# The output product of a hybrid conv/attention layer as seven block products per pair of token tiles

## The chip, the cores and the metric

One core of one Trainium2 chip. The metric is the device time of the whole program in microseconds, here the median of three runs. The engines are called as in the profile: PE (TensorE, with PEld for its weight loads), DVE (VectorE), ACT (ScalarE), POOL (GpSimd) and SP (SyncE, which issues most DMAs).

## The reference, cut to what matters

A decoder layer for 1024 tokens of width 1024, in float32. Two branches, a causal convolution and a dilated window attention of 24 heads, are gated and merged, and one output product brings them back to the residual stream.

```python
merged = jax.nn.sigmoid(g_conv) * y_conv + jax.nn.sigmoid(g_att) * y_att   # y_att = (att * silu(z_att)) @ w_att_out
x = x + gate * (merged @ w_o[layer])                                      # 1024 x 1024 x 1024
return _rmsnorm(x, final_g)
```

## The kernel before

All products are made on PE in three matmuls with two-part operands: each float32 operand is split into a high part (`hi`, ACT rounds it to the matmul type) and a low part (`lo`, the rest, by a subtraction on DVE or POOL), and hi.hi, hi.lo and lo.hi are summed in PSUM (`mm3`, L72 to L75). A "group" of twelve such matmuls is four 128-row steps of the contraction at 512 columns.

The program runs in stages. A first stage makes modulation and the first projections. A second makes the other projections, the convolution and its output; there many projections are made in pairs by `strassen` (L703 on), a two by two block product with seven block products for eight: four sums of weight blocks are made by POOL, the sums of the other operand (`t_hi`, `t_lo`) stand ready, and each product's result is passed on by ACT copies from bank to bank. This stage follows an order written out by hand: in each step stand PE's group, then ACT's copies (rank COPY), evictions (EVICT) and high pieces (HIGH), then POOL's pieces (POOLED), then DVE's work on results (POST_), then loads (LOAD). `at(step, rank, fn)` puts work into it. Within a step the ranks come in that order, and within a rank what was put in first comes first. Every engine has its own queue and takes its instructions in the order in which they are written there, the stage's loop being within `tc.manual_schedule`.

The attention stage is likewise written out in slots. One slot is twelve matmuls of a projection (queries, keys, then the last gates) with the attention's own scores, transposes and value products between them; slots -11 to -1 hold projections alone. `move_kq` (L1263) copies query and key parts with DMAs issued by SP into one tile per head; the scores of the first heads are in slot 0. Work beside it stands in `beside`, by slot: loading values, combining the three groups of heads (`combine`), splitting the first blocks of `w_o` (`w_out`) and of `w_att_out` (`first_ao`). `oc` tiles (four buffers) hold the attention's results. The last act ahead of attention is to store `gate_c` as a row (`gscr`, 1024 elements of 4 bytes).

The last stage is not written out in steps before the change; its order is the planner's, by the order of the program. For each of eight tiles `d` of the merged features, `project` makes two groups with the attention output (`ah`, `al`) as the right operand and `w_att_out`'s split columns as the left one; DVE multiplies with the gate `sgr` (Sigmoid by ACT), adds `ttr` (the convolution's share), and the sum is split into `hh[:, d]` (ACT) and `hl[:, d]` (DVE). Then each of eight token tiles `t` gets its 1024 output columns in two halves: `out_cols` makes 24 matmuls over eight contraction steps, DVE multiplies with `gate_b` and adds the tokens' `x`, ACT squares and sums. `out_norm` then works out the row's scale (three small DVE operations, a square root on ACT, five small ones on DVE) and scales two halves, which SP stores. The last tile's second half is done in two quarters of 256 columns.

## Time and profile before

| | us |
|---|---|
| median of 3 runs (1207.93 to 1208.35) | 1208.23 |
| the profiled execution | 1208.01 |
| its span, first to last instruction | 1206.2 |
| merge with the attention output, from PE's first matmul to the output's first | 1067.43 to 1110.95 |
| output product, to PE's last matmul | 1110.95 to 1198.18 |
| end of the span | 1206.2 |

Times in the profile count from the first instruction. A row of the order of time is: start, duration, engine, line, operation, what is written from what, sizes, count, and in brackets how long the engine was idle ahead of it and what released it. A "q" behind an engine is its sequencer, which issues DMAs. The rows of stages give the length, then each engine's busy time and instructions, the granted share of PE's clock, the DMA engines' busy share and the GB/s moved. A row of DMA issues gives count, KB each, and the median time from issue to landing.

### The profile page before, as it was taken

What the parts mean: (1) busy time and instruction counts of PE and PEld (TensorE: products, weight loads), DVE (VectorE), ACT (ScalarE), POOL (GpSimd) and SP (SyncE); (2) the same over time, 40 slices, a digit from 0 to 9 for tenths busy, and PEclk for the clock granted to TensorE, in tenths of its full rate; (3) what the DMA queues carried; (4) which work ended last, traced back from release to release, by engine and by line L of the source; (5) the groups of instructions that cost most, each with busy time, mean ns of one, the idle gap of its engine ahead of it and who ended that gap; (6) DMA issues with size and microseconds to landing.
All of it is one profiled execution on the core that took longest, in us unless ns stands there. A gap on an engine that the chain in (4) does not pass through costs nothing.

```text
span 1206.2 us, 17336 instructions
## 1 busy us (share of the span) xinstructions
PE 1189.1 (99%) x6042; PEld 996.1 (83%) x6042; DVE 905.1 (75%) x1488; ACT 586.7 (49%) x1213; POOL 429.2 (36%) x316
## 2 busy tenths in 40 slices
PE   9999999999999999999999999999999999999997
PEld 7787888888888888788888888888888888888886
DVE  7879999999999998796346657867877852649444
ACT  5655244545444443741126656656656664445111
POOL 0005867787787874672321111111111111200000
PEclk9999999999999999999999999999999999999999
DMA  9685333313233147666855455665666563768232
GB/s 358 192 300 175 105 106 122 101 66 105 100 100 131 63 140 274 226 201 235 225 135 149 111 144 130 181 174 141 180 168 146 145 191 124 234 228 281 87 105 70
DMA packets 100141, 194.49 MB, mean 161 GB/s; under 512 B 29587, under 2 KB 43219, under 8 KB 100054
## 3 DMA queue, kind: packets, MB, share of 16 engines
q1 hardware_dynamic: 83376, 186.77, 50.4%
q10 hardware_dynamic: 16678, 6.61, 2.0%
q8 instruction: 48, 0.79, 0.3%
q14 instruction: 39, 0.32, 0.1%
HBM read 122.25 MB, written 39.62 MB: 134 GB/s over the span
## 4 chain that ended last, share of the span: by engine, by line
PE 90%; DVE 3%; ACT 2%; DMA 2%; issue 1%; POOL 1%; SPq 0%; DVEq 0%; ACTq 0%; POOLq 0%
PE d L73 23%; PE d L74 23%; PE d L75 23%; PE o L1370 4%; PE d L603 4%; PE s L1333 3%; PE t L1349 3%; PE d L1661 2%; PE d L1662 2%; PE d L1663 2%; DMA wraw<-in_w_v 1%; PE d L274 1%; ACT hh L238 1%; DVE hl L241 1%; DVE tot L788 1%
## 5 line engine op out<-in xcount | busy, mean ns | idle before, releaser
L545 DVE SCALAR_TENSOR_TENSOR acc<-u,cw,acc 128x1024 f32<-128x1024 f32 x232 | 298.8, 1288 | 6.6
L73 PE MATMUL d<-hh,whi 128*128 128x512 f32 x752 | 295.0, 392 | 2.2 <-ACT gs L1023 2.2
L74 PE MATMUL d<-hl,whi 128*128 128x512 f32 x752 | 293.4, 390 | 0.0
L75 PE MATMUL d<-hh,wlo 128*128 128x512 f32 x752 | 293.3, 390 | 0.0
L456 POOL TENSOR_TENSOR wlo<-wraw,whi 128x512 fp32r<-128x512 f32 x130 | 175.8, 1362 | 216.4 <-ACT whi L453 216.2
L58 POOL TENSOR_TENSOR wlo<-wraw,whi 128x512 fp32r<-128x512 f32 (+1 forms) x56 | 82.9, 1498 | 366.5 <-ACT whi L57 362.5
L75 PEld LDWEIGHTS d<-hh,wlo 128*128 128x128 f32 x752 | 141.2, 188 | 30.2
L73 PEld LDWEIGHTS d<-hh,whi 128*128 128x128 f32 x752 | 141.4, 188 | 29.1 <-ACT gs L1023 2.7
L74 PEld LDWEIGHTS d<-hl,whi 128*128 128x128 f32 x752 | 141.4, 188 | 25.9
L453 ACT ACTIVATE whi<-wraw 128x512 fp32r<-128x512 f32 x130 | 79.1, 624 | 86.9 <-DMA wraw<-in_w_co 26.1
L1342 ACT ACTIVATE sb<-sb,stats 128x128 f32<-128x128 f32 (+1 forms) x192 | 84.8, 443 | 31.2 <-DVE stats L1338 30.9
L1338 DVE CUSTOM_DVE_ANT_0 sb<-s,mask 128x128 f32<-128x128 f32 (+1 forms) x192 | 59.7, 349 | 52.9 <-PE s L1333 51.5
L1349 PE MATMUL t<-ident,sb 128*128 128x128 f32 x280 | 73.7, 276 | 0.0
L1370 PE MATMUL o<-ph,vt 128*64 128x128 f32 (+1 forms) x432 | 65.9, 253 | 0.0
L1164 ACT ACTIVATE ph<-t 128x384 fp32r<-128x384 f32 (+2 forms) x96 | 45.6, 475 | 38.9 <-PE t L1349 25.8
L1167 DVE TENSOR_TENSOR pl<-t,ph 128x384 fp32r<-128x384 f32 (+2 forms) x96 | 52.0, 541 | 10.8 <-ACT ph L1164 10.2
L1333 PE MATMUL s<-k,ql 128*128 128x128 f32 (+1 forms) x192 | 55.0, 292 | 0.0
L1164 ACT ACTIVATE kqp<-rot 128x512 fp32r<-128x512 f32 x24 | 23.1, 964 | 64.4 <-DVE rot L1187 39.0
L1370 PE MATMUL o<-pl,vt 128*64 128x128 f32 (+1 forms) x216 | 52.8, 261 | 0.0
L1661 PE MATMUL d<-oh,hh 128*128 128x512 f32 (+1 forms) x136 | 51.2, 377 | 0.0
L1663 PE MATMUL d<-oh,hl 128*128 128x512 f32 (+1 forms) x136 | 51.2, 377 | 0.0
L73 PE MATMUL d<-uh,whi 128*128 128x512 f32 x128 | 50.0, 390 | 1.2 <-ACT gs L612 1.2
(300 smaller groups left out, 2640.2 us busy)
## 6 DMA issues: line engine op xcount, KB each, us to landing
wraw<-in_w_t SPq DMA_DIRECT2D x67, 512.0 KB, 4.2
k<-kqp SPq DMA_DIRECT2D x96, 128.0 KB, 2.3
q<-kqp SPq DMA_DIRECT2D x96, 128.0 KB, 2.3
wraw<-in_w_v SPq DMA_DIRECT2D x19, 512.0 KB, 4.5
wa<-in_w_ada SPq DMA_DIRECT2D x16, 512.0 KB, 5.8
ql<-kqp SPq DMA_DIRECT2D x48, 128.0 KB, 2.3
wg<-wscr SPq DMA_DIRECT2D x48, 128.0 KB, 3.2
hscr<-x SPq DMA_DIRECT2D x8, 512.0 KB, 3.4
```

Source lines behind the costliest of these rows:

```text
L58: (lo_eng or nc.vector).tensor_sub(lo, raw, hi.bitcast(F32))
L73: nc.tensor.matmul(ps, lh, rh, start=start, stop=False, skip_group_check=again)
L74: nc.tensor.matmul(ps, lh, rl, start=False, stop=False, skip_group_check=again)
L75: nc.tensor.matmul(ps, ll, rh, start=False, stop=stop, skip_group_check=again)
L453: nc.scalar.activation(self.hi, src(), AF.Copy)
L456: nc.gpsimd.tensor_sub(self.lo, src(), self.hi.bitcast(F32))
L545: nc.vector.scalar_tensor_tensor(acc, u[:, k:k + S], cw[:, ct, k:k + 1], acc, op0=mult, op1=add)
L1333: products.append((w, lambda c=c, w=w, l=x[:, ts_], r=k[:, ks], i=i: nc.tensor.matmul(ps[:, c:c + w], l, r, start=i == 0, stop=i == 1)))
L1342: nc.scalar.activation(sb[:, c:c + w], sb[:, c:c + w], AF.Exp, bias=stats[:, t, h, 1:2], scale=-1.0, accum_out=stats[:, t, h, 0:1])
L1349: yield from ((lambda c=c: nc.tensor.transpose(ps[:, c:c + P], sb[:, c:c + P], ident)) for c in range(0, o, P))
L1370: nc.tensor.matmul(out_, l, r, **kw))
L1661: nc.tensor.matmul(ps, hh[:, k, c], rh, start=k == 0, stop=False)
```

## The change

The last stage becomes a second run of the hand-written steps (`serve_steps`, the old loop as a function). Steps 0 to 15 are the merge's groups, as before in count, but the merged features are kept whole in `merged[0]` and `merged[1]` and not split. Steps 16 to 43 are four pairs of token tiles (t, t + 4), each with seven block products of twelve matmuls in place of eight: blocks are two tiles of tokens by two halves of the contraction by two halves of the columns. The sums of merged blocks are made in place, in the first pair by DVE, in the others by POOL, and split piece by piece (`Form2`). The four sums of `w_o` blocks are made early in attention (`out_combos`: loads, one DVE, three POOL operations, one ACT negation, stores to `tscr`, for each of two halves), loaded again in the merge and split by ACT and POOL into `hh` and `hl`. Two blocks of `w_o` are split late, in steps 16 and 17 (`late_b`). In attention the fourth block of `w_o` is now split as well (slot 113), and the first two column blocks of `w_att_out` are loaded.

```diff
+    def out_combos(c):
+        t = b11, b12, b22, b21 = [ap_.tile([P, S], F32, name="oc", tag="oc", bufs=4) for _ in range(4)]
+        for x, n, kp in zip(t, (0, 1, 1, 0), (c, c, 2 + c, 2 + c)):
+            nc.sync.dma_start(x, a["w_o"][n, kp])
+        nc.gpsimd.tensor_sub(b11, b11, b12)
+        yield
+        nc.vector.tensor_sub(b12, b12, b22)
+        nc.gpsimd.tensor_add(b22, b22, b11)
+        nc.gpsimd.tensor_sub(b21, b21, b22)
+        yield
+        for x, i in ((b11, 0), (b12, 2)):
+            nc.sync.dma_start(tscr[i][c], x)
+        yield
+        nc.scalar.activation(b22, b22, AF.Copy, scale=-1.0)
+        for x, i in ((b22, 1), (b21, 3)):
+            nc.sync.dma_start(tscr[i][c], x)
         yield
...
-                  (110, w_out(0, 2)), (111, first_ao())):
+                  (110, w_out(0, 2)), (111, first_ao()), (113, w_out(0, 3))):
         in_steps(it, [x, x + 2])
+    in_steps(out_combos(0), [-11, -8, -4, -2])
+    in_steps(out_combos(1), [-1, 2, 4, 6])
...
+    def merge(d, half):
+        s = cols_of(half)
+        ps = bank()
+        for k in range(4):
+            c = slice(k * P, (k + 1) * P)
+            mm3(ps, ao[d].hi[:, c], ao[d].lo[:, c], ah[k][:, s], al[k][:, s], k == 0, k == 3)
+
+        def post():
+            m = merged[d // 4][:, d % 4, s]
+            nc.vector.tensor_mul(sg[d][:, s], ps, sg[d][:, s])
+            nc.vector.tensor_add(m, m, sg[d][:, s])
+        at(now[0], POST_, post)
...
+        at(max(2 * d - 2, -1), LOAD, lambda d=d: sg_load(d))
+        at(max(2 * d - 4, -1), LOAD, lambda d=d: merged_load(d))
+        at(2 * d, EVICT, lambda d=d: nc.scalar.activation(sg[d], sg[d], AF.Sigmoid))
...
+    for step, i, c, tag in ((0, 1, 0, "wlo"), (1, 1, 1, "wlo"), (3, 2, 0, "wraw"), (5, 2, 1, "wraw"), (7, 3, 0, "wlo"),
+                            (9, 3, 1, "wlo"), (11, 4, 0, "wraw"), (12, 4, 1, "wraw")):
+        combo(step, i, c, tag)
+
+    def late_b(step, c):
...
+        def high():
+            woh[1, 2 + c], wol[1, 2 + c] = (head_tile(x, "oh") for x in (("k0", "k1"), ("k2", "q0"))[c])
+            nc.scalar.activation(woh[1, 2 + c], raw[0], AF.Copy)
+        at(step, LOAD, load)
+        at(OUT + c, HIGH, high)
+        at(OUT + c, POOLED, lambda: nc.gpsimd.tensor_sub(wol[1, 2 + c], raw[0], woh[1, 2 + c].bitcast(F32)))
+
+    for c in range(2):
+        late_b(13 + 2 * c, c)
...
+    def out_pair(p):
+        step = OUT + 7 * p
+        rows = [slice(t * P, t * P + P) for t in (p, p + 4)]
+        a11, a12, a21, a22 = (merged[kh][:, :, r] for r in rows for kh in range(2))
...
+            def __init__(self, n, src, high_at, low_at, eng):
+                def high():
+                    tag = ("wlo", "wlo", "whi", "whi", "wraw", "wraw", "wraw")[n]
+                    Pieces.__init__(self, wpool.tile([P, 1024], F32R, name="wf", tag=tag,
+                                                     bufs=3 if tag == "wraw" else 2))
+                    nc.scalar.activation(v(self.hi), src(), AF.Copy)
+                at(high_at, HIGH, high)
+                at(low_at, POST_ if eng is nc.vector else POOLED,
+                   lambda: eng.tensor_sub(v(self.lo), src(), v(self.hi).bitcast(F32)))
...
+        if first_:
+            f11 = Form2(0, lambda: a11, 12, 12, P_)
+            at(step - 1, POST_, lambda: D_.tensor_add(v(s1), a21, a22))
+            fs1 = Form2(1, lambda: v(s1), step, step, D_)
+            at(step, POST_, lambda: D_.tensor_add(a21, a21, a11))
+            at(step, POST_, lambda: D_.tensor_add(a11, a11, v(s1)))
+            fs2 = Form2(2, lambda: a11, step + 1, step + 1, D_)
+            f12 = Form2(3, lambda: a12, step + 1, step + 1, D_)
+            at(step + 1, POOLED, lambda: P_.tensor_add(v(s4()), a12, a11))
+            fs3 = Form2(4, lambda: a21, step + 2, step + 2, D_)
+            fs4 = Form2(5, lambda: v(s4()), step + 3, step + 3, P_)
+            f22 = Form2(6, lambda: a22, step + 4, step + 4, P_)
+        else:
+            at(step - 3, POOLED, lambda: P_.tensor_add(v(s1), a21, a22))
+            f11 = Form2(0, lambda: a11, step - 3, step - 2, P_)
+            at(step - 2, POOLED, lambda: P_.tensor_add(a21, a21, a11))
+            at(step - 2, POOLED, lambda: P_.tensor_add(a11, a11, v(s1)))
+            fs1 = Form2(1, lambda: v(s1), step - 2, step - 1, P_)
...
+            f22 = Form2(6, lambda: a22, step + 3, step + 4, P_)
...
+        t1, t2 = p, p + 4
+        end = p == 3
+        at(step, COPY, copy("b", "a"))
+        at(step + 1, COPY, copy("x", "g", 1.0, 0))
+        at(step + 2, COPY, copy("d", "b", -1.0))
+        at(step + 3, POST_, lambda: gated(t1, 0, 0, 512, box["a"]))
+        at(step + 4, COPY, copy("y", "d", 1.0, 1))
+        at(step + 5, POST_, lambda: gated(t2, 1, 512, 1024, box["g"], ((box["y"], box["g"]), sub)))
+        at(step + 5 + (not end), POST_, lambda: gated(t1, 1, 512, 1024, box["b"], ((box["b"], box["x"]), add)))
+        at(step + 5 + 2 * (not end), POST_, lambda: out_norm(t1, 2))
...
+        at(step + 6, POST_, whole)
+        at(step + 6 + (not end), POST_, lambda: out_norm(t2, 3 if end else 2))
+        groups.extend([g0, g1, more("b", fs2, combo_block(2)), more("a", f12, b_block(0, 1)),
+                       more("d", fs3, combo_block(3)), more("b", fs4, b_block(1, 1)),
+                       last if end else more("d", f22, combo_block(4))])
```

`gated` is two DVE operations (multiply with `gate_b`, add to `x` in place), three where a result is first the sum or difference of two, and ACT's sum of squares. `last` makes the last block product in two halves of 256 columns, and `whole` for the last pair takes each half by itself.

More of the change, by code (lines that the diff above doesn't have):

```diff
@@ L102, in layer @@
     vcscr = [dram.tile([P, S], F32, name=f"vcscr{j}") for j in range(KT)]
+    tscr = [[dram.tile([P, S], F32, name=f"tscr{i}{c}") for c in range(2)] for i in range(4)]
     szscr = [dram.tile([P, S], F32, name=f"szscr{j}") for j in range(KT)]
@@ new lines, in layer, with ao_load, ao_high @@
+    ao = {0: Pieces(ahead_ao[0])}
+    raw_ao = {d: ahead_ao[1][:, d * 512:d * 512 + 512] for d in range(2)}
+    def ao_load(d, tag):
+        raw = in_half(tag, "raws")
+        for i in range(2):
+            raw_ao[d + i] = raw[:, i * 512:i * 512 + 512]
+            nc.sync.dma_start(raw_ao[d + i], a["w_ao"][d + i])
+    def ao_high(d):
+        late = {2: hh[:, 6], 3: hh[:, 7], 4: hl[:, 6], 5: hl[:, 7]}
+        ao[d] = Pieces(late[d] if d in late else wpool.tile([P, 1024], F32R, name="whi", tag="whi"))
+        ao[d].high(raw_ao[d])
@@ new lines, in layer @@
+    for d in range(KT):
+        for half in (range(2) if d < KT - 1 else (1, 0)):
+            groups.append(lambda d=d, half=half: merge(d, half))
+        at(max(2 * d - 2, -1), LOAD, lambda d=d: sg_load(d))
+        at(max(2 * d - 4, -1), LOAD, lambda d=d: merged_load(d))
+        at(2 * d, EVICT, lambda d=d: nc.scalar.activation(sg[d], sg[d], AF.Sigmoid))
+    at(-1, LOAD, lambda: ao_load(2, "gate_b"))
+    at(-1, LOAD, lambda: ao_load(4, "fg_b"))
+    at(5, LOAD, lambda: ao_load(6, "gate_b"))
@@ L1695 @@
+    for p in range(4):
+        out_pair(p)
+    serve_steps(groups)
 def kernel(**inputs):
```

259 lines of the change are left out of this document (160 added, 99 removed).

## The prediction

> **What bounds the kernel now.** I read the page first: its busy shares and the chain that ended last. Then the busy time by stage, TensorE's order of time at the stage borders, and last the other engines' order of time where the change puts work.
>
> ```profile
> span 1206.2 us, 17336 instructions
> PE 1189.1 (99%) x6042; PEld 996.1 (83%) x6042; DVE 905.1 (75%) x1488; ACT 586.7 (49%) x1213; POOL 429.2 (36%) x316
> PE 90%; DVE 3%; ACT 2%; DMA 2%; issue 1%; POOL 1%; SPq 0%; DVEq 0%; ACTq 0%; POOLq 0%
> L73 PE MATMUL d<-hh,whi 128*128 128x512 f32 x752 | 295.0, 392 | 2.2 <-ACT gs L1023 2.2
> ```
>
> TensorE (PE) is the chain. What it does not have to do comes off the time, and every wait put on it is paid in full.
>
> ```profile
> core 0: us, PE busy (x) PEld busy (x) DVE busy (x) ACT busy (x) POOL busy (x), PEclk, DMA share, GB/s
> 1067.43:1110.95 43.52, 43.52 (x194) 36.04 (x192) 34.16 (x53) 25.57 (x35) 0.00 (x0) 1.00 0.89 304
> 1110.95:1195.42 84.47, 84.47 (x385) 70.44 (x384) 42.85 (x100) 15.28 (x41) 0.00 (x0) 1.00 0.28 93
> ...
> 1110.95 0.39 PE L1661 MATMUL d<-oh,hh 128*128 128x512 f32 x1
> 1195.42 0.28 PE L1661 MATMUL d<-oh,hh 128*128 128x256 f32 x1
> ```
>
> The first row is the merge with the attention output (192 matmuls), the second the output product up to its last 24 pieces. In the new stage groups 0 to 15 are merge and 16 to 43 are the four pairs' seven block products each. Both have no idle PE. 43.52 us / 192 = 0.2267 us from matmul to matmul (a matmul's own 0.39 us overlaps the next), so a group of twelve is 2.72 us.
>
> **The change, part by part.**
>
> *Fewer products.* From 1067.43 to the start of the last 24 half-width pieces at 1195.42 PE now takes 127.99 us. Afterwards there lie 16 merge groups and 27 of 28 block groups before the last, again halved, group: 43 x 2.72 = 116.96 us. **-11.03 us**. I call the start of that last group T.
>
> *Waits in the first token pair.* The steps are written out in order: in each, PE's group, then ACT's COPY, then its HIGH pieces. Rows of two earlier stages price this.
>
> ```profile
> 205.24 0.39 PE L73 MATMUL d<-hh,whi 128*128 128x512 f32 x1
> 205.44 0.60 ACT L736 ACTIVATE sd<-d 128x512 f32<-128x512 f32 x1 [1.60 <-PE d L75]
> 205.93 0.62 ACT L453 ACTIVATE whi<-wraw 128x512 fp32r<-128x512 f32 x1
> ...
> 346.16 1.28 POOL L456 TENSOR_TENSOR wlo<-s,whi 128x512 fp32r<-128x512 f32 x1
> 347.49 0.50 PE L75 MATMUL d<-t1h,wlo 128*128 128x512 f32 x1 [0.20 <-POOL wlo L456]
> 347.83 0.40 PE L73 MATMUL d<-t1h,whi 128*128 128x512 f32 x1
> 348.06 0.39 PE L74 MATMUL d<-t1l,whi 128*128 128x512 f32 x1
> ...
> 1057.75 1.06 ACT L1164 ACTIVATE oh<-wraw 128x1024 fp32r<-128x1024 f32 x1 [0.40 <-ACT gs L1204]
> 1058.71 0.62 ACT L1164 ACTIVATE whi<-wraw 128x512 fp32r<-128x512 f32 x1
> 1067.45 0.63 ACT L57 ACTIVATE whi<-wraw 128x512 fp32r<-128x512 f32 x1 [1.41 <-PE d L74]
> 1068.11 0.69 DVE L58 TENSOR_TENSOR wlo<-wraw,whi 128x512 fp32r<-128x512 f32 x1 [0.81 <-ACT whi L57]
> ```
>
> ACT sat 1.60 us for PE at the copy and only then ran the piece written behind it: it keeps the written order. In step 16 of the new stage that order is: copy of `a` into `b` (waits for group 16), `late_b(0)`'s 1024-wide piece, then `fs1`'s high piece. Group 17, next on PE, needs `fs1`. Counted from the moment G when group 17 could start: copy at G+0.20 (205.44 against 205.24), next instruction +0.49, behind the 1024-wide piece +0.96, DVE's low piece +0.66, its end +0.69 = G+3.00. The group's first two matmuls read the high piece and can go earlier; the third needs the low one. A late low piece costs as in the rows at 347.49: PE goes 0.05 after it (346.16+1.28), and the next matmul is 0.34 behind instead of 0.23. The third would have been at G+0.45, so the group ends 3.05-0.45+0.11 = 2.71 us late. Step 17 repeats it: copy of `g`, `late_b(1)`, `fs2`, then DVE; group 18 needs `fs2`. **+5.42 us** for the two. If matmuls waited for the whole tile it would be 0.9 more; if ACT's order were otherwise, 0. Groups 19 to 22 have their pieces: `f12` is done with `fs2`; `fs3` is ready 2.0 us after group 18, needed after 2.7.
>
> *GpSimd before the second pair.* `f22`'s high piece stands behind the copy of `d` in step 20, and six GpSimd operations follow, the last the low piece of the second pair's `fs1`.
>
> ```profile
> 206.05 1.29 POOL L710 TENSOR_TENSOR s<-wraw 128x512 f32<-128x512 f32 x1
> 211.18 1.30 POOL L456 TENSOR_TENSOR wlo<-s,whi 128x512 fp32r<-128x512 f32 x1
> ```
>
> Four starts apart, (211.18-206.05)/4 = 1.28 us each. From step 20's start: 2.72+0.20+0.49+0.63 = 4.04, six operations to 11.7; group 24's third matmul is due at 4 x 2.72+0.45 = 11.33. **+0.5 us** (0, to 1.9 if each took a fifth longer, an estimate). Later pairs put `f22` four microseconds earlier and do not meet this.
>
> *The clock.* Each of those waits leaves PE idle for 2.1 us (G+0.23 to G+2.3) and thin for 0.7 more.
>
> ```profile
> 493.84:497.25 3.41, 3.05 (x22) 2.84 (x22) 1.01 (x5) 1.50 (x4) 2.67 (x2) 1.00 0.94 314
> 497.25:500.67 3.42, 3.42 (x11) 2.64 (x10) 0.34 (x2) 1.88 (x4) 1.97 (x2) 0.50 0.96 369
> ```
>
> This is the one drop of the granted clock inside the trace: after a stretch of 3.41 us with one gap and a few tiny matmuls (x22 in all) the next 3.42 us ran at 0.50, which costs up to 1.7 us. I take one drop out of two waits: **+1.7 us** (0 to 3.4). The Trainium skill (TensorE: Matmul & The Clock Gate, "Why this matters for your kernels") allows gaps up to about 3 us: only "One MID window of idle" brings half clock. By that rule neither wait would drop it and the sum would be 1.7 lower. The trace's drop came with PE at work for part of the window, so the row speaks against a rule that wants it wholly idle.
>
> *The tail.* In the last pair DVE's order is: the gated block of tile 7, the one of tile 3, tile 3's whole norm, then only the two halves that PE finishes last.
>
> ```profile
> 1187.31 0.69 DVE L1664 TENSOR_TENSOR y<-d,gate_b 128x512 f32<-128x512 f32 x1 [4.02 <-PE d L1663]
> 1188.03 0.69 DVE L1665 TENSOR_TENSOR y<-y,xt 128x512 f32<-128x512 f32 x1
> 1189.51 0.16 DVE L1672 TENSOR_TENSOR r<-ss 128x1 f32<-128x1 f32 x1 [0.79 <-ACT xt L1666]
> 1191.16 1.41 DVE L1679 SCALAR_TENSOR_TENSOR y<-y,r,fg_b 128x512 f32<-128x512 f32 x2
> ...
> 1192.32 0.39 PE L1663 MATMUL d<-oh,hl 128*128 128x512 f32 x1
> 1192.75 0.69 DVE L1664 TENSOR_TENSOR y<-d,gate_b 128x512 f32<-128x512 f32 x1 [0.17 <-PE d L1663]
> ...
> 1198.50 0.42 DVE L1664 TENSOR_TENSOR y<-d,gate_b 128x256 f32<-128x256 f32 x1 [1.26 <-PE d L1663]
> 1198.95 0.42 DVE L1665 TENSOR_TENSOR y<-y,xt 128x256 f32<-128x256 f32 x1
> 1199.95 0.16 DVE L1674 TENSOR_TENSOR r<-r,ss 128x1 f32<-128x1 f32 x1 [0.57 <-ACT xt L1666]
> ```
>
> Tile 3's `b` is done with group 42: DVE follows its last matmul by 0.43 (1192.32 to 1192.75), T+0.20. Three dependent operations 0.72 apart (1187.31 to 1188.03) put the add at T+1.64; the sum of squares is read 1.48 later (T+3.12); the norm takes 3.06 (1189.51 to 1192.57): T+6.18. Then two multiplies and two adds of 256, 0.45 apart, last add at T+7.53; 1.00 to the sum, and 6.25 from there to the end of the span (1199.95 to 1206.2): T+14.78. Now it is 1206.2-1195.42 = 10.78. **+4.00 us**.
>
> *Attention.* Added: eight loads and eight stores of 512 KB, two 1024-wide operations on DVE, six on GpSimd, two on ACT, all early; `w_o`'s fourth block is split inside attention instead of behind it. PE waits for none of it as long as the first heads' moves keep their reserve (rival below). Taken at 0 (0 to 3.4).
>
> *Merge.* DVE loses the splits. The loads grow to 31 of 512 KB, 16.3 MB in about 46 us; the merge row shows 304 GB/s at a DMA share of 0.89, 342 at full share, 47.5 us. So gates come up to 2 us late, but eight banks let PE run eight groups (21.8 us) ahead of DVE, and weights lead by four groups. At the start the second weight tile's piece stands behind the first Sigmoid; 0, at most the 2.2 us that the L73 row lost at its one such place.
>
> **Sum.** -11.03+5.42+0.5+1.7+4.00 = +0.6 on the profiled execution's 1208.01 (span 1206.2 and 1.81 around it), 1208.6; the median of the runs shown is 0.22 above that execution: **1208.8 us**, no change.
>
> **Rivals.**
>
> *Faster, the waits do not come:* ACT takes the pieces before the copies, or the groups find them ready. 1208.8-5.42-1.7 = **1201.7 us**. Against it: the 1.60 us in the row at 205.44, with the piece behind it.
>
> *The clock holds in both waits* (above): 1208.8-1.7 = **1207.1 us**, inside the forecast case, with a quarter of its chance, since the one drop seen does not say how idle a window must be.
>
> *Slower, attention's start:*
>
> ```profile
> cscr<-gs SPq DMA_DIRECT2D x2, 256.0 KB, 9.6
> gscr<-gate_c SPq DMA_DIRECT2D x1, 4.0 KB, 11.8
> ql<-kqp SPq DMA_DIRECT2D x4, 128.0 KB, 2.3
> 613.23 0.69 DVE L1167 TENSOR_TENSOR kqp<-rot,kqp 128x512 fp32r<-128x512 f32 x1 [0.70 <-ACT kqp L1164]
> 615.96 0.69 DVE L1167 TENSOR_TENSOR kqp<-d,kqp 128x512 fp32r<-128x512 f32 x1 [2.04 <-ACT kqp L1164]
> 623.95 0.59 SPq L1263 DMA_DIRECT2D ql<-kqp  x1
> 631.46 0.22 PE L1333 MATMUL s<-k,q 128*128 128x128 f32 x1
> ```
>
> The first four weight loads (2.1 MB, 6.1 us at 342 GB/s) stand behind the stores and the 4-byte scatter of `gate_c`, which lands only after 11.8 us. If they land past 614, DVE's subtraction, written ahead of the low piece at 613.23, holds it to 616. The moves behind it go 2.8 us later, with two stores (about 1 us of SP's queue, as its issues beside them, and 3.1 us of DMA) put before the second ones: 6.9 against a reserve of 631.46-(623.95+2.3) = 5.2. PE waits 1.7 us, and as much again where the second set does it in slot 2: **1212.2 us**. It decides when the subtraction waits over 1 us. For it: the 11.8. Against it: DVE's idle 2.04 behind, and the loads may get past the scatter.
>
> That the products do not get fewer is excluded by the listing: seven groups of twelve matmuls per pair; and the block products of the earlier stage run at the same spacing (347.83 to 348.06).
>
> **How the numbers follow.** Forecast case 0.55, its own range 1206.3 to 1211.8 (clock 0 to 3.4, GpSimd 0 to 1.8, the whole-tile wait); faster rival 0.25; slower rival 0.20. A run tells 0.2% (2.4 us) from nothing. Of the forecast case 0.40 lies within that, 0.13 above, 0.02 below: faster 0.27, same 0.40, slower 0.33. The range 1201.5 to 1213.0 takes in both rivals' values.
>
> **What would show it.** In the changed profile: 16 merge groups without a gap, then two gaps of some 2 to 3 us on PE in the first pair, released by ACT and DVE; a third below 1 us at group 24; the clock at 0.50 once behind them; from PE's last matmul to the end about 4 us more than now, with DVE in tile 3's norm when PE stops; no PE gap in attention. A first pair without gaps makes me wrong by 5 to 7 us; a gap at the first scores by 2 to 4.

## The result, and the profile after

The changed kernel takes 1240.6 us (median of four runs, 1237.3 to 1243.4), the kernel before beside it 1208.1: ratio 1.0268, 95% interval 1.0238 to 1.0297. The prediction was 1208.8. The profiled executions took 1237.34 us (span 1235.5) and 1208.01 (span 1206.2), 29.3 apart in span. Runs disturbed as a whole are left out of all comparisons; the profile of one run below (the sums alone, first time) was such a one, at 3088 us, and is not read.

Three lines of the changed kernel's page: span, busy shares, chain.

```profile
span 1235.5 us, 17394 instructions
PE 1190.4 (96%) x5982; PEld 991.9 (80%) x5982; DVE 943.6 (76%) x1478; ACT 608.0 (49%) x1249; POOL 538.7 (44%) x376
PE 76%; DMA 6%; DVE 5%; POOL 4%; issue 4%; ACT 3%; SPq 1%; DVEq 0%; POOLq 0%; ACTq 0%
```

TensorE has 60 matmuls fewer (5982 for 6042), but of the chain it holds 76% where it held 90%. Busy time by stage of the changed kernel: first scores to merge, merge, output blocks up to the last matmul, tail.

```profile
631.81:1075.00 443.19, 438.00 (x2709) 379.17 (x2708) 294.82 (x781) 263.69 (x705) 78.46 (x51) 1.00 0.62 169
1075.00:1118.52 43.52, 43.52 (x193) 36.06 (x192) 29.76 (x28) 19.83 (x24) 28.85 (x14) 1.00 0.92 338
1118.52:1222.84 104.32, 87.98 (x348) 68.64 (x347) 75.40 (x103) 39.99 (x84) 66.49 (x41) 0.89 0.24 84
1222.84:1235.52 12.68, 0.28 (x3) 0.07 (x1) 6.72 (x23) 1.98 (x8) 0.00 (x0) 0.68 0.22 83
```

The merge is as long as before (43.52). The output stage has 104.32 us in place of 87.23, although 28 groups need only 28 x 2.72 = 76.2: 28.1 us are waits and half clock. Attention is 7.2 us longer (443.19 for 435.97), the tail 4.6 (12.68 for 8.04). With 0.4 at the first scores that is 7.2+17.1+4.6+0.4 = 29.3.

By groups (from first matmul to first matmul, less 2.72) the 28.1 us lie at 16 to 18 (15.2), 24 (4.3 with its neighbour), 33 and 34 (3.7), 38 to 41 (4.8). TensorE's waits by what ended them (total, times, longest), from 600 us on:

```profile
PE d L75 <- DVE wf L1821: 5.5, 2, 4.1
PE t L1351 <- DVE pl L1169: 4.9, 2, 4.1
PE d L73 <- ACT wf L1818: 4.9, 2, 2.7
PE d L75 <- POOL wf L1821: 3.4, 3, 2.1
PE d L73 <- ACT d L1855: 2.5, 3, 1.3
PE d L75 <- POOL wlo L58: 2.3, 1, 2.3
```

`wf` are the pieces of the block products and `d` from ACT the copies: 16.3 us of waits in the output stage. What that stage lost beyond them is mostly the clock, below. `pl` lies in attention, where TensorE was also busy 2.0 us longer at half clock (438.00 for 435.97). `wlo` came near 621, ahead of the first scores. That these are only 0.4 us late is luck: the half clock that the trace of before has at 497.25 did not come in this execution. One hundred matmuls ahead of the first scores it lay 2.2 us in front (606.55 for 608.79), and it lost 2.6 us from there on.

### The profile page after: what moved, and what is told of

It reads as the page before. It is cut to its first block, busy times and chain, and to the rows that moved or that the text cites. A ratio compares the mean times of both kernels' runs of the same rounds, so it can differ in the third digit from the quotient of the medians.

```text
span 1235.5 us, 17394 instructions
## 1 busy us (share of the span) xinstructions
PE 1190.4 (96%) x5982; PEld 991.9 (80%) x5982; DVE 943.6 (76%) x1478; ACT 608.0 (49%) x1249; POOL 538.7 (44%) x376
## 4 chain that ended last, share of the span: by engine, by line
PE 76%; DMA 6%; DVE 5%; POOL 4%; issue 4%; ACT 3%; SPq 1%; DVEq 0%; POOLq 0%; ACTq 0%
PE d L75 20%; PE d L73 20%; PE d L74 20%; PE d L604 6%; PE o L1372 4%; PE s L1335 3%; PE t L1351 2%; POOL wf L1821 2%; DMA sgr<-ascr 1%; DVE merged L1692 1%; DMA oc<-in_w_o 1%; DMA ascr<-gs 1%; DMA wraw<-in_w_t 1%; DMA x<-in_xT 1%; DMA tscr<-oc 1%
## 5 line engine op out<-in xcount | busy, mean ns | idle before, releaser
L73 PE MATMUL d<-hh,whi 128*128 128x512 f32 x752 | 295.7, 393 | 2.5 <-ACT gs L1024 2.2
L73 PEld LDWEIGHTS d<-hh,whi 128*128 128x128 f32 x752 | 141.7, 188 | 29.6 <-ACT gs L1024 2.7
L1335 PE MATMUL s<-k,q 128*128 128x128 f32 (+1 forms) x192 | 51.3, 273 | 0.0
L73 PE MATMUL d<-uh,whi 128*128 128x512 f32 x128 | 50.0, 390 | 1.2 <-ACT gs L613 1.2
L604 PE MATMUL d<-whi,hh 128*128 128x512 f32 x128 | 50.5, 394 | 0.0
```

The costliest lines, as they stand in the source:

```text
L73: nc.tensor.matmul(ps, lh, rh, start=start, stop=False, skip_group_check=again)
L604: nc.tensor.matmul(ps[i], l[:, k, c], r, start=k == 0 and n == 0, stop=k == KT - 1 and n == 2)
L1335: products.append((w, lambda c=c, w=w, l=x[:, ts_], r=k[:, ks], i=i: nc.tensor.matmul(ps[:, c:c + w], l, r, start=i == 0, stop=i == 1)))
```

## The experiments

Five theories: A, ACT's written order in steps 16 and 17 (the prediction's); B, DVE and GpSimd hold each other up; C, the early sums block queues at attention's start; F, the square root of a pair's second norm stands ahead of ACT's copies; G, the same of ACT's squares. The table has the profiled executions: start of the merge; what is lost from there to the last group beyond 2.72 us a group; tail. The merge of kernels with the same attention began at 1075.0 to 1081.6, so that column is good to some 6 us, the other two to about 1. A part of this scatter is a wait for `pl` near 985 that some executions have and others not: e14, whose attention is that of the kernel before, loses 5.2 us there, e13 5.1, the changed kernel 1.0, the kernel before nothing. A profiled execution can lie 4 us off the median of its kernel; e12's is the fastest of twelve (1204.7).

| run | time | ratio (95%) | merge begins | lost in groups | tail |
|---|---|---|---|---|---|
| before | 1208.1 | | 1067.4 | 0 | 8.0 |
| after | 1240.6 | 1.0238-1.0297 | 1075.0 | 28.1 | 12.7 |
| e1, e13 sums alone | 1218.7, 1220.9 | 1.0052-1.0100, 1.0063-1.0125 | 1082.7 (e13) | 1.7 (e13) | 8.0 |
| e2 ACT's order | 1235.4 | 1.0189-1.0237 | 1080.8 | 20.4 | 12.9 |
| e3 GpSimd quiet | 1236.2 | 1.0194-1.0241 | 1077.9 | 24.8 | 12.5 |
| e4 both | 1228.4 | 1.0139-1.0219 | 1077.6 | 15.8 | 13.2 |
| e6 second norm later | 1247.3 | 1.0294-1.0335 | 1081.3 | 32.7 | 13.2 |
| e11 and squares later | 1245.1 | 1.0262-1.0320 | 1081.6 | 30.4 | 12.9 |
| e7 tail | 1241.0 | 1.0227-1.0276 | 1077.8 | 30.9 | 11.6 |
| e5 sums on DVE | 1250.1 | 1.0317-1.0356 | 1088.3 | 25.7 | 13.1 |
| e10 sums at the end | 1243.6 | 1.0260-1.0323 | 1068.8 | 37.9 | 12.8 |
| e8 together | 1236.3 | 1.0204-1.0242 | 1085.7 | 17.2 | 11.8 |
| e9 second version | 1221.4 | 1.0091-1.0130 | 1069.8 | 15.5 | 12.1 |
| e12 third version | 1208.8 | 0.9981-1.0002 | 1069.6 | 1.4 | 12.2 |
| e15 last version | 1206.0 | 0.9949-0.9980 | 1069.0 | 5.3 | 10.5 |
| e14 GpSimd beside | 1234.7 | 1.0189-1.0218 | 1072.6 | (other kernel) | 8.0 |

### The first pair: e2, e3, e4

Order of time on ACT, on DVE and on GpSimd around group 17 of the changed kernel:

```profile
1118.08 1.06 ACT L1700 ACTIVATE sgr<-sgr 128x1024 f32<-128x1024 f32 x1 [3.49 <-DMA sgr<-ascr]
1119.04 1.99 ACT L1715 ACTIVATE hh<-wt 128x1024 fp32r<-128x1024 f32 x2
1121.44 0.58 ACT L1855 ACTIVATE d<-d 128x512 f32<-128x512 f32 x1 [0.40 <-PE d L75]
1121.93 1.05 ACT L1731 ACTIVATE oh<-wt 128x1024 fp32r<-128x1024 f32 x1
1123.45 0.63 ACT L1818 ACTIVATE wf<-s 128x512 fp32r<-128x512 f32 x1 [0.47 <-DVE s L1829]
```

```profile
1120.62 2.74 DVE L1829 TENSOR_TENSOR s<-merged,merged 128x512 f32<-128x512 f32 x1
1123.28 0.68 DVE L1691 TENSOR_TENSOR sgr<-d,sgr 128x512 f32<-128x512 f32 x1
1123.99 2.13 DVE L1692 TENSOR_TENSOR merged<-merged,sgr 128x512 f32<-128x512 f32 x1
1126.04 2.82 DVE L1821 TENSOR_TENSOR wf<-s,wf 128x512 fp32r<-128x512 f32 x1
```

```profile
1120.16 5.41 POOL L1716 TENSOR_TENSOR hl<-wt,hh 128x1024 fp32r<-128x1024 f32 x2 [1.64 <-ACT hh L1715]
1125.53 2.79 POOL L1734 TENSOR_TENSOR oh<-wt,oh 128x1024 fp32r<-128x1024 f32 x1
```

ACT's order is the predicted one: copy, 1024-wide piece, `fs1`. But the piece then waits another 0.47 us for the sum `s`, and DVE, which should need 0.69 for each of its operations, takes 2.74, 2.13 and 2.82 for three of them, all with two inputs in SBUF and all beside GpSimd's large subtractions; the one with an input in PSUM (`d`) takes 0.68. And the last gate came late (ACT's Sigmoid waited 3.49 us for its load), so that DVE began late. The third matmul of group 17 started at 1128.92. With 0.69 for each of the three operations, the low piece of `fs1` would by these rows have ended near 1124.2, late gate or not (an estimate); group 17 could start at 1121.24, so that is the prediction's G+3.00. It ended at 1128.86.

e2, theory A:

```
-            fs1 = Form2(1, lambda: v(s1), step, step, D_)
+            fs1 = Form2(1, lambda: v(s1), step, step, D_, EARLY)     # fs2 in the same way
-        at(OUT + c, HIGH, high)                                     # late_b, and its low piece
+        at(OUT + 2 + c, HIGH, high)
```

> The changed kernel with another written order on ScalarE in steps 16 and 17: the high pieces of fs1 and fs2 stand ahead of the copy that waits for TensorE, and the two 1024-wide pieces (late_b) come two steps later. Theory A, ScalarE's order makes the loss of 15.3 us in groups 17 and 18: 9 to 13 of it go, time 1228 to 1232 against 1240.6. Theory B, VectorE and GpSimd holding each other up makes most of it: 2 to 5 go, 1236 to 1239. Groups 24, 34 and 41 keep their 4 us each under both.

e3, theory B (the same in `late_b`, for steps 18 and 19):

```
-        at(step + 3, POOLED, lambda: nc.gpsimd.tensor_sub(hl[:, n], ...))   # the last sum's two
+            last_in((14, 17)[c], lambda: nc.vector.tensor_sub(hl[:, n], ...))
```

> The changed kernel with the low pieces of the last sum (two) and of late_b (two) made by VectorE, behind its other work of steps 14 and 17 to 19, so that GpSimd has next to nothing in steps 14 to 17; ScalarE's order is as in the changed kernel. Theory B: VectorE's adds and low pieces go from 2.1 to 2.8 us back to 0.69, and 6 to 10 of the 15.3 us in groups 17 and 18 go: 1231 to 1235. Theory A: the waits stay, 0 to 3 go: 1238 to 1241.

e4, both edits:

> Both edits together. If A and B between them are the cause, groups 17 and 18 lose under 3 us in place of 15.3: 1227 to 1229. If the gate that comes late from DRAM sets group 17 (ScalarE's last sigmoid waited 3.49 us for it), some 4 us of it stay: 1230 to 1233.

Groups 16 to 18 lose 15.2 us in the changed kernel, 6.7 in e2, 12.9 in e3, 5.9 in e4; over all groups the losses fall by 7.7, 3.3 and 12.3. e2 stayed below the nine of theory A and e3 below the six of theory B; e3's 2.3 us in groups 16 to 18 are what A had foretold for it. And e2 is not A alone, since GpSimd's low pieces of `late_b` move away from group 17 with ACT's. B's price itself did go in e3, on DVE as foretold; what ate the gain is the last gate, on ACT:

```profile
1128.64 0.69 DVE L1835 TENSOR_TENSOR s<-merged,merged 128x512 f32<-128x512 f32 x1
```

```profile
1123.96 1.06 ACT L1700 ACTIVATE sgr<-sgr 128x1024 f32<-128x1024 f32 x1 [5.07 <-DMA sgr<-ascr]
```

This Sigmoid started 46.0 us after the merge's start, in the changed kernel 43.1. Besides, e3 and e4 gave DVE a low piece in step 14 whose high piece ACT makes only behind that Sigmoid, and the gate's multiplication stands behind it: it starts 2.2 us after the Sigmoid's end (1127.19 in e3, 1124.41 in e4), in the changed kernel at once. So A and B are both at work, but these runs do not divide the 15.2 us between them. In e4 5.9 us stay, as the expectation's second half had it, though the time, 1228.4, lies in the range of its first.

### The price of DVE and GpSimd together: e14

```
+        for _ in range(4):
+            nc.gpsimd.tensor_sub(probe[0], probe[0], probe[0])     # in out_cols of the kernel before
```

> The kernel before with 68 subtractions of a 128x512 tile from itself on GpSimd, which nothing needs, beside merge and output stage: the disputed price by itself. Theory B (GpSimd and VectorE hold each other up where both read two operands from SBUF): VectorE's y<-y,xt goes from 0.69 to between 1.2 and 2.2 us in the mean, its y<-d,gate_b with one operand from PSUM stays at 0.69, GpSimd's own operation goes from 1.28 to 1.5 to 1.8. TensorE has all its data early there, so the time stays within 3 us of 1208. Rival (VectorE is slow through DMA writes or ScalarE): both stay at 0.69.

GpSimd could start on these subtractions as soon as their tile was there, and did at 1058.9. So most of the 68 ran beside the merge, and `y<-y,xt` of the output product, which the expectation names, met few (723 ns in the mean there). The merge has an operation of the same kind, `ttr<-ttr,sgr`. DVE's operations by line (count | busy us, mean ns) in the merge of the kernel before, then of e14, then e14's on GpSimd:

```profile
L1633 DVE TENSOR_TENSOR sgr<-d,sgr 128x512 f32<-128x512 f32 x15 | 9.9, 685 | 3.5 <-ACT sgr L1618 3.5
L1634 DVE TENSOR_TENSOR ttr<-ttr,sgr 128x512 f32<-128x512 f32 x14 | 9.2, 684 | 0.0
```

```profile
L1634 DVE TENSOR_TENSOR ttr<-ttr,sgr 128x512 f32<-128x512 f32 x12 | 17.6, 1487 | 0.0
L1633 DVE TENSOR_TENSOR sgr<-d,sgr 128x512 f32<-128x512 f32 x12 | 7.9, 678 | 3.6 <-ACT sgr L1618 3.6
```

```profile
L1660 POOL TENSOR_TENSOR probe<-probe 128x512 f32<-128x512 f32 x44 | 59.4, 1350 | 3.5
```

The operation with both inputs in SBUF goes from 684 to 1487 ns; the one that reads `d` from PSUM stays (685, 678). GpSimd loses little in the mean (1350 ns, not the 1.5 to 1.8 us expected; 1.28 us was the row in the prediction). So B's price on DVE is shown by itself. What I had expected of the time was wrong: 1208 within 3, and it is 1234.7. The kernel before was not safe from it, since DVE, which makes the merge's weight pieces, was busy for 34.16 of its 43.52 us: slowed down, it became the bound there. TensorE waited 12.3 us for its `wlo`, and 5.6 at the start of the output product for `hh` and `hl`.

The Trainium skill (SBUF — State Buffer, "SBUF: two separate sides") gives the reason: the port pair that the two engines share is "an exclusive lock, not a bandwidth split", held for a whole instruction, and on DVE's side an operation with two SBUF inputs wants it when GpSimd's reads SBUF. The rows agree: two SBUF inputs 684 to 1487 ns, one of two in PSUM 685 to 678.

### Groups 33 to 42: e6 and e11

ACT and DVE ahead of group 34 of the changed kernel:

```profile
1186.41 0.20 ACT L113 ACTIVATE tmp<-r 128x1 f32<-128x1 f32 x1 [4.71 <-DVE r L1780]
1186.52 0.58 ACT L1855 ACTIVATE xy<-d 128x512 f32<-128x512 f32 x1
```

```profile
1181.93 1.05 DVE L115 TENSOR_TENSOR tmp<-tmp 128x1 f32<-128x1 f32 x1
1183.02 1.21 DVE L116 TENSOR_TENSOR tmp<-tmp,r 128x1 f32<-128x1 f32 x1
```

ACT stood 4.71 us at the square root of the second tile's norm; the copy behind it was due long before. DVE had been held up in the first tile's norm, even in operations on one column, 1.05 and 1.21 us for what takes 0.16.

```
-        at(step + 6 + (not end), POST_, lambda: out_norm(t2, 3 if end else 2))
+        at(step + (6 if end else 9), POST_, lambda: out_norm(t2, 3 if end else 2))
```

> The changed kernel with the norm of each pair's second tile two steps later (three pairs), so that ScalarE's square root for it no longer stands ahead of the copies of the next pair. Theory F (that square root, waiting 4.7 us for VectorE, makes the waits at groups 33, 34, 40 and 41): 5 to 7 of their 7.8 us go, 1233 to 1236. Rival (GpSimd's chain of pieces alone makes them late): the waits stay, 1240.

The waits at 33, 34, 40 and 41 went as F says; but new ones came at 28, 31, 35, 36 and 42, 11.6 us from 28 to 42 in place of 8.5, and the time is 1247.3 (in the profile 6.3 us of that lie ahead of the merge, in the scatter above). F names the wait and not the cause: the next thing on ACT that waits for DVE took its place. e11 moves that too, the squares:

```
+        if t % 4 < 3:
+            at(now[0] + 1, POST_, square)      # the sum of squares of gated, one step later
```

> The run with the second norm later, and now the squares of the first three pairs one step later too (and with them the first tile's norm). Theory G: in the run before it ScalarE's squares, which wait for VectorE's adds that GpSimd stretches to 1.66 us, stood ahead of the copies in place of the square root; the waits at groups 28 to 42 (11.3 us there, 8.5 in the changed kernel) fall to 2 to 4, time 1236 to 1240 with that run's other waits. Rival: the copies are late through the pieces (GpSimd): 9 to 12 us stay, 1245 to 1248.

Groups 28 to 36 then lose nothing; 6.1 us stay at 37 to 42, most of them at 42, in the last pair, whose squares were not moved. G holds for the pairs in which it was tried; in all, groups 28 to 42 fall from 11.6 to 6.1 us and not to the 2 to 4 expected. The time (1245.1, interval overlapping e6's) does not show it, since the first pair lost 3 us more and the rest of the runs scatters.

### Attention: e1, e13, e5, e10

SP's queue in the changed kernel, what ACT then waits for, what TensorE waits for, SP's raw weights in the kernel before, and GpSimd and TensorE ahead of the first scores:

```profile
631.30 0.80 SPq L1534 DMA_DIRECT2D tscr<-oc  x2
632.15 5.85 SPq L1522 DMA_DIRECT2D oc<-in_w_o  x4
638.05 0.90 SPq L62 DMA_DIRECT2D wraw<-in_w_t  x2
```

```profile
645.77 0.63 ACT L57 ACTIVATE whi<-wraw 128x512 fp32r<-128x512 f32 x1 [5.21 <-DMA wraw<-in_w_t]
```

```profile
649.76 0.30 PE L1351 MATMUL t<-ident,sb 128*128 128x128 f32 x1 [4.09 <-DVE pl L1169]
```

```profile
629.42 1.23 SPq L62 DMA_DIRECT2D wraw<-in_w_t  x2
```

```profile
617.58 2.37 POOL L1527 TENSOR_TENSOR oc<-oc 128x1024 f32<-128x1024 f32 x1
621.21 0.50 PE L75 MATMUL d<-hh,wlo 128*128 128x512 f32 x1 [2.26 <-POOL wlo L58]
```

SP sends its DMAs in the order written. The second set's loads need buffers that the first set's stores must leave first; SP stood 5.85 us over four of them, and the heads' raw weights went out at 638.05 in place of 629.42. ACT, in order too, stood 5.21 us at their split with the softmax pieces behind it, so TensorE waited 4.09 us at the transposes. Ahead of the first scores it waited another 2.26 us for GpSimd, whose split stood behind its sum `oc<-oc`. This wait came in each of the six other executions with the same attention (2.29 to 3.60 us in e2, e3, e4, e6, e7 and e11), in five of them with half clock behind it, and their first scores came at 634.8 to 638.5 (before 631.46).

e1 is the kernel before with nothing but `out_combos` and its slots; e13 is the same once more.

> The kernel before, with nothing of the change but the early sums of output weights in attention (their loads, their adds on GpSimd, VectorE and ScalarE, their stores); the sums are then not used. Theory C, the sums delay attention (SyncE's queue holds the next raw weights behind the sums' stores and loads, GpSimd's split waits behind the sums): attention is 7.6 us longer, the time is 1215 to 1217. Rival: attention is longer through the other edits there (output weights split earlier, the wider first w_ao tile): 1208.

> The run of the early sums alone once more, for its trace (the first one's profiled execution lay at 3088 us, with every matmul at twice its length). Theory C: PE waits near 618 and 645 as in the changed kernel, the merge begins 7 to 11 us later than in the kernel before (1067.4), merge and output stage are as before: 1215 to 1219. Rival, that the sums' data traffic lengthens the later stages: merge and output stage longer than 43.5 and 87.2.

The sums alone cost 0.5 to 1.3%, about 10 us (1218.7 beside 1209.0, 1220.9 beside 1209.2): C, both a little above their ranges. In e13 the same two waits come (2.3 us at GpSimd's split, 2.1 at `pl`), and merge and output stage stay within 1.8 us. Its merge begins 15.2 us late and not 7 to 11: 5.1 of them are lost near 985, in the wait that e14 has without any sums.

e5 makes all sums on DVE and finishes both sets ahead of the raw weights:

```
-        nc.gpsimd.tensor_add(b22, b22, b11)
+        nc.vector.tensor_add(b22, b22, b11)       # and so for all four, and the sign
-    in_steps(out_combos(1), [-1, 2, 4, 6])
+    in_steps(out_combos(1), [-6, -4, -3, -2, -1])
```

> The changed kernel with the early sums of weights made by VectorE alone (the sign too, which ScalarE changed) and their stores and the second set's loads done before SyncE comes to the raw weights of the heads. Theory C (GpSimd's sums ahead of its split, SyncE's queue ahead of the raw weights): PE's waits of 2.65 us near 618 and 4.31 us near 645 go, from the first scores to the merge it is again 436 us in place of 443, time 1232 to 1234 against 1240.6. Rival: the weight traffic itself delays the heads' weights wherever the sums are made: the waits stay within 2 us, 1238 to 1241.

```profile
PE d L73 <- DVE kqp L1169: 15.5, 3, 12.6
```

This wait of e5 is neither theory's: DVE took SP's place. Its sums stood at the head of its queue for loads that SP could issue only at 633.56, and `kqp`, which TensorE needed, stood behind them; the time lies above both ranges. What C says of the time after that holds: from first scores to merge 438.2 us (before 436.0, after 443.2).

e10 puts the sums where DVE and GpSimd have room, in attention's last slots, in half tiles:

```
-    in_steps(out_combos(0), [-11, -8, -4, -2])     # and set 1
+    for c in range(2):
+        for h in range(2):
+            in_steps(out_combos(c, h), [100 + 8 * c + 2 * h + x for x in (0, 2, 3, 4)])
```

> The changed kernel with the early sums made in attention's last 17 slots, in half tiles, by VectorE, in buffers that the scores no longer need; its start is then as in the kernel before. Theory C (the place of the sums, in the queues of SyncE, GpSimd and VectorE where attention starts, costs the time): PE's waits near 618 and 645 go, the merge begins at 1067 to 1070 in place of 1075, time 1232 to 1236. Rival (the traffic costs it wherever it is): the wait moves to the last slots, the merge begins at 1073 to 1076, time 1238 to 1242.

The merge begins at 1068.8, as C says (100 matmuls ahead of the first scores this execution, too, was 1.9 us in front), but then groups 0 to 2 lose 5.5 us: the last set's traffic holds up SP's last loads, ACT stands behind them with a gate, and TensorE waits 2.0 us for it (`PE d L73 <- ACT gs`). The rival is right for the second set; the first set costs nothing that shows in this place. Groups 16 to 18 lose 18.7 us, and the time, 1243.6, lies above both ranges.

### The tail: e7

e7 joins the last pair's two norms in one chain, and lets other engines have a part of the scaling:

```
+            at(step + 4, POOLED, lambda: ahead_of_norm(t1, 0))      # tile 3 times fg_b, on GpSimd
-        at(step + 6 + (not end), POST_, lambda: out_norm(t2, 3 if end else 2))
+        at(step + 6 + (not end), POST_, lambda: out_norms(p, end) if end else out_norm(t2, 2))
+                if end and t == p:                                  # in out_norms
+                    nc.scalar.activation(xs[t][:, s], xs[t][:, s], AF.Copy, scale=q)
```

> The changed kernel with another end: in the last pair VectorE takes the last quarters before any norm, both tiles' norms are one chain on columns of two, and tile 3 is multiplied by the final gain ahead on GpSimd and scaled on ScalarE. If VectorE's order is the whole of the longer tail: 8.5 to 9 us from the last matmul to the end in place of 12.7 (before: 8.0), time 1236 to 1237. If the two tiles' work is simply more: 11 to 12, time 1239.

11.6 us in place of 12.7: the rival. Both tiles' work stands behind each other on DVE whichever comes first. The trace also has GpSimd's multiplication beside DVE's last quarters (an add of 256 columns took 1.20 us in place of 0.42), and a wait that the changed kernel has too: DVE waits for ACT's squares, because ACT writes them over the block of which DVE has still to read the other half. In the changed kernel's order of time on DVE it is this line:

```profile
1227.94 0.42 DVE L1769 TENSOR_TENSOR s4y<-d,gate_b 128x256 f32<-128x256 f32 x1 [0.66 <-ACT d L1771]
```

e15, below, writes these squares elsewhere, and the wait is gone.

### Together: e8, e9, e12, e15

e8 has e4's edits (with the loads that can wait issued after the last gate's), e5's sums, one norm chain for both tiles one step later (the expectation says two), e7's tail, and in pairs 2 to 4 the first sum and the first low piece on DVE.

> All edits in one: sums on VectorE early, first pair as in the run with both edits but with the loads that are not urgent issued behind the last gate's, one norm chain for both tiles and two steps later, the first two piece operations of pairs 2 to 4 on VectorE in place of GpSimd, the other tail. If the waits named are all there are: attention -7, first pair -13, group 24 -3, groups 33 to 41 -7, tail -4 from 1240.6: 1205 to 1208, level with or just below the kernel before. If the groups move their waits to the next piece instead: 1212 to 1220.

Its 1236.3 us lie above both ranges. It loses e5's 13 us in attention; in the output stage, as in e6, waits came at 28, 31, 32, 38 and 39. ACT (its short rows that read out a sum of squares are not shown) and TensorE there:

```profile
1157.82 0.60 ACT L1780 ACTIVATE d<-xt 128x512 f32<-128x512 f32 x1 [2.17 <-DVE xt L1779]
1159.34 0.60 ACT L1780 ACTIVATE d<-xt 128x512 f32<-128x512 f32 x1 [0.80 <-DVE xt L1779]
1159.97 0.58 ACT L1872 ACTIVATE d<-d 128x512 f32<-128x512 f32 x1
```

```profile
1160.60 0.50 PE L73 MATMUL d<-hh,wf 128*128 128x512 f32 x1 [2.22 <-ACT d L1872]
```

The copy `d<-d`, for which TensorE waits, stands behind two squares, and these behind DVE's adds. From this came theory G.

e9 is e8 with e10's sums, made on DVE, and e11's squares:

```
-    in_steps(out_combos(0), [-11, -9, -8, -7, -7])                  # and set 1
+            in_steps(out_combos(c, h), [100 + 8 * c + 2 * h + x for x in (0, 2, 3, 4)])
+        if t % 4 < 3:
+            at(now[0] + 1, POST_, square)
```

> The run with all edits together, with the sums at attention's end, the squares a step later, the first pair's first low piece on VectorE, and a tail in which one half of tile 3 alone is multiplied ahead. If C, B, F and G name all the waits: the merge begins at 1067 to 1070, the output stage loses 3 to 6 us over its 116.96, the tail is 9.5 to 10.5: 1203 to 1208, faster than before by up to 0.4%. If the first pair's data still come late through the DMA queues: 1208 to 1214.

Groups 22 to 30 lose nothing now; 6.3 us are lost at the merge's start, 4.9 in groups 16 to 18, and the time, 1221.4, lies above both ranges. e12 then took the first set of sums early again, stored sooner, and the second into slots 100 to 106; the third sum's low pieces to DVE; the next pair's first operations a step earlier:

```
-            at(step - 3, POOLED, lambda: P_.tensor_add(v(s1), a21, a22))
-            f11 = Form2(0, lambda: a11, step - 3, step - 2, P_)
-            at(step - 2, POOLED, lambda: P_.tensor_add(a21, a21, a11))      # and a11
+            at(step - 4, POOLED, lambda: D_.tensor_add(v(s1), a21, a22))
+            f11 = Form2(0, lambda: a11, step - 4, step - 4, D_, low_rank=POOLED)
+            at(step - 3, POOLED, lambda: P_.tensor_add(a21, a21, a11))      # and a11
```

> The version with all edits once more: the first set of sums early again (its last sum on VectorE, stored sooner), the second set at attention's end in its first six slots; the low pieces of the third sum on VectorE so that GpSimd is quiet from the merge's last groups on; the next pair's first sum and pieces one step earlier; pair 3's norms behind the last pair's first gated block. If the waits left in the version before have the causes read there: the merge begins at 1068 to 1070 and loses nothing (6.3 before), groups 16 to 18 lose 0 to 2 (4.9 before), the tail is 9.5 to 10.5 (12.1 before): 1204 to 1209, level with the kernel before or faster by up to 0.4%. If the DMA queues of the merge are the bound whatever VectorE does: groups 16 and 17 keep 4 to 5, 1210 to 1213.

e12 by stage, the merge and the output blocks:

```profile
1069.63:1113.15 43.52, 43.52 (x193) 36.05 (x192) 32.13 (x33) 20.44 (x24) 21.43 (x11) 1.00 0.89 321
1113.15:1190.73 77.58, 76.53 (x348) 63.47 (x347) 69.03 (x89) 38.66 (x79) 47.33 (x31) 1.00 0.35 122
```

The output stage takes 77.58 us, 1.4 above its matmuls, in place of 104.32, at full clock. So the gain of the products is there: 87.23-77.58 = 9.65 us. What ate it in this execution is the tail (+4.2; 12.2 and not the 9.5 to 10.5 expected) and attention (+2.2). That leaves 3.3 us, and this execution is the fastest of its twelve: in the median the time is that of the kernel before within 0.2%.

e15 changes four places of e12: the first set's stores on ACT's queue and a step later, one sum of pairs later, the squares of tile 7 into another tile, and no multiplication on GpSimd in the tail (not shown: a 1024-wide low piece of weights one step later, one norm product of pair 3 ahead of the last norm, and the second halves of the last stores on ACT's queue):

```
-            nc.sync.dma_start(tscr[i][c], x)
+            nc.scalar.dma_start(tscr[i][c], x)
-    in_steps(out_combos_early(0), [-11, -8, -5, -4])
+    in_steps(out_combos_early(0), [-11, -8, -5, -2, -1])
-            at(step + 1, POOLED, lambda: P_.tensor_add(v(s4()), a12, a11))
+            at(step + 2, POOLED, lambda: P_.tensor_add(v(s4()), a12, a11))
+            junk = late["xy"][:, c0:c1] if t == 7 and c1 <= 512 else ps
-            at(step + 4, POOLED, lambda: ahead_of_norm(t1, 0))
```

> The version before (1208.8 against 1209.2) with three last edits: the early set's stores issued by ScalarE and its last sum two slots later (SyncE issued the first head's rows 2.4 us late); in the first pair GpSimd's sum and VectorE's first large piece moved from between the second form's adds and its low piece (group 18 lost 1.4); in the tail no multiplication on GpSimd, one of pair 3's norm products in VectorE's wait for the last square, and the last squares not written over the block that VectorE still reads. If these readings are right: attention -1 to -2, group 18 -1.3, tail -1.5 to -2.5 from 12.2: 1203 to 1205.5, faster than before by 0.3 to 0.5%. If the tail is bound by VectorE's sum of work wherever it stands: 1206 to 1207.5.

e15 takes 1206.0 us beside 1209.5: ratio 0.9965, interval 0.9949 to 0.9980, so faster than both kernels, by a third of a percent over the kernel before. Its profiled execution shows the tail at 10.5 and not lower, and loses 4.1 us in groups 16 and 17 (5.3 in all), which its edits had not been made for: the gates' loads landed later there. The reading on the tail came true, and that on group 18 too (no loss); attention shows no gain (438.8 us from scores to merge). The time fell between the two ranges, just above the one that was hoped for.

## Where the prediction was wrong

Of the 28.7 us between the forecast for the profiled execution (1208.6) and its 1237.34, 20.5 lie in the output stage up to the last group, 7.6 ahead of the merge and 0.6 in the tail.

*Fewer products, -11.03:* right. 540 matmuls follow the merge's start where 600 did, and e12 shows the time.

*Waits in the first pair, +5.42:* right in place, order and releaser, too small by 9.8 us: groups 16 to 18 lost 15.2, in four waits of 2.73, 4.05, 2.15 and 1.45 us (10.4) and the half clock behind them. The working took DVE's 0.69 us as a constant and the sum `s` as ready. Three of DVE's operations took 2.1 to 2.8, and the last gate came late from a merge whose DMA share was 0.92. That gates would come up to 2 us late stood in the paragraph on the merge, with DVE's distance from TensorE as cover; at the merge's end this cover ends, since the sum of the next product needs DVE's result at once.

*GpSimd ahead of group 24, +0.5 (0 to 1.9):* 3.9, a wait of 2.05 us and the half clock behind it. I took 1.28 us for an operation; beside a busy DVE most take 1.62 to 1.82. The bound of a fifth had no row behind it.

*Later pairs, nothing:* 8.5 us in groups 33 to 42, two stretches of half clock among them. I had looked at what each product needs and not at what stands in ACT's queue ahead of its copies.

*The price of engines beside each other* is the step that failed in all three: the prediction took DVE's 0.69 us and GpSimd's 1.28 as they are when the other rests, and beside each other they took up to 2.82 and 1.82. The trace of before had it, on DVE and on GpSimd at attention's end, and I read such groups' means as mixtures of shapes:

```profile
1038.98 2.78 DVE L1451 TENSOR_TENSOR wg<-wg 128x512 f32<-128x512 f32 x1
1041.80 0.69 DVE L1454 TENSOR_TENSOR wg<-wg,gt 128x512 f32<-128x512 f32 x1
```

```profile
1038.17 3.05 POOL L58 TENSOR_TENSOR wlo<-wraw,whi 128x1024 fp32r<-128x1024 f32 x1 [8.94 <-ACT whi L57]
```

In the old merge and output stage GpSimd was busy for 0.00 us, in the new ones for 28.85 and 66.49: the durations that I took from there were those of a DVE alone.

*Clock, one drop, +1.7:* there were five stretches at half clock in the output stage. TensorE was busy for 18.5 us in them, so they cost about 9.2 (an estimate). Two of them with the stretch before:

```profile
1186.42:1189.83 3.41, 1.89 (x7) 0.95 (x7) 3.01 (x7) 2.75 (x6) 2.13 (x2) 1.00 0.55 207
1189.83:1193.24 3.41, 3.41 (x9) 2.64 (x9) 1.88 (x3) 0.72 (x2) 3.41 (x3) 0.50 0.38 103
1210.32:1213.73 3.41, 1.45 (x6) 0.60 (x4) 3.09 (x7) 2.66 (x6) 2.22 (x2) 1.00 0.55 204
1213.73:1217.14 3.41, 3.41 (x10) 2.64 (x9) 1.80 (x3) 0.72 (x2) 2.97 (x2) 0.50 0.21 79
```

TensorE was busy for 1.89 and 1.45 us of the 3.41 us before, and the next 3.41 us ran at 0.50, nine or ten matmuls in place of 15. Its waits there were 0.86 and 0.67 us, and 1.28 and 0.68: two short waits close together were enough. The Trainium skill's rule (TensorE: Matmul & The Clock Gate, "Why this matters for your kernels"), an idle window, would have let neither of these two drop; the rows decide against it.

*The tail, +4.00:* 4.6, with DVE in tile 3's norm when TensorE stopped, as foretold. The missing 0.66 is the wait for ACT's squares.

*Attention, 0 (0 to 3.4):* 7.2 us behind the first scores, 1.0 of them the wait near 985, and 2.6 ahead of them, which the 631.81 hides; some 10 in e1 and e13. So the slower rival was right that the sums delay the first scores (by 3.9 to 6.6 us in the six other executions), and wrong in how: TensorE waited for GpSimd's split behind a sum, not for SP's moves behind DVE's subtraction. I had counted SP's issues at 0.5 us each, and not that an issue can stand in the queue for a buffer, with the weights of the next head behind it.

*Merge, 0:* right (43.52 us).

*The range of the forecast case*, 1206.3 to 1211.8, does not follow from its terms: clock 0 to 3.4, GpSimd 0 to 1.8 and the whole-tile 0.9 give 1206.6 to 1212.7. The result lies far outside either.

## What to carry to other kernels

When work moves to an engine that was idle, take the durations of its neighbours anew: where VectorE and GpSimd both read two operands from SBUF, bound each by a row in which the other was at work. An engine that works in order passes every wait on; ask of each copy that the critical engine needs what stands ahead of it in its queue, and move whatever waits for a late engine behind it, all of it, since taking one away only lets the next one through. Prefetched work is free only if its issues, too, find their buffers empty.

## What had not been expected of the hardware

Operations on one column (128x1) with two SBUF inputs are held up by a busy GpSimd as wide ones are: 1.05 to 1.24 us in place of 0.16. Those with one input are not: a reciprocal of the same chain took 0.16 beside it (at 1181.73). 68 useless subtractions on GpSimd made the kernel before 25 us slower, although VectorE's share of the span was 75% there.
